# Both attention sections put in the order of the program text on all five engines of an encoder kernel

## The chip, the core and the metric

The kernel runs on one core of one Trainium2 chip. The core has five engines with an instruction queue each: TensorE (PE, matmuls and transposes), VectorE (DVE), ScalarE (ACT), GpSimd (POOL) and SyncE (SP, which here does nothing but issue DMAs). Each engine has one queue, and in the trace its instructions start in the order in which the built program has them, so that one that waits for another engine or for a DMA holds up all that stand behind it. The metric is the time of one execution on the device in microseconds (us); lower is better.

## What is computed

Two encoder layers over 1024 tokens of width 1024, and a last RMSNorm. Cut to what matters here:

```python
h = rmsnorm(x, g)
q, k, v, ..., gate = split(h @ w_in)                 # one input projection for all head groups
# layer 0: 6 windowed heads (A), 6 dense heads with rotary positions (B), 4 heads into 256 memory tokens (X)
# layer 1: 6 differential heads (C), 4 memory heads (X)
p  = softmax(q @ k.T / 8 + bias);  y = p @ v         # A (with a sink logit), B, X
p1, p2 = softmax(q1 @ k1.T / 8 + bias), softmax(q2 @ k2.T / 8 + bias)
y  = rmsnorm((p1 - lam * p2) @ v) * c                # C
out = x + (concat(y) * silu(gate)) @ w_out
```

All of it is float32; the kernel splits operands into a high and a low part and sums matmuls of the parts, three for a projection.

## The kernel before

The kernel is written with a recording layer that builds a program, knows which instruction reads and writes which buffer, puts the instructions of each engine in an order by its own estimate of when each is ready, and adds the waits. The order of the program text binds it only where two instructions share data. A buffer tag has a fixed number of slots; a new buffer waits until the slot's last readers are done.

The attention of each layer is a list of steps, one for 128 query rows of a head (256 rows for A): in layer 0 8 X steps, 8 B steps of the first head, then 64 steps of B and A in a pattern that is mostly B, B, A; in layer 1 8 X steps and 6 times 8 C steps. `run_steps` writes them as a software pipeline:

```python
for i in range(n + LAG + 1):
    hooks(i)                          # layer 1, C steps: Early.step(), one piece of w_out
    steps[i - 1].hop()                # DMA er<-e: step i-1's softmax copied to a buffer of rounded words
    finish = steps[i].s1()            # PE scores (sb, sa, sc); DVE minimum (mn, or e and mn); ACT exp
    jobs.pull(...)                    # 8 matmuls of a projection (acc, or pre) for each pull; weights of the next job loaded
    ...                               # posts of a C pair: ssqc, then rbcc
    steps[p3].s3()                    # on every second step: PE probabilities by values (ob, oa, oc)
    steps[p2].s2()                    # two or three steps behind: PE transposes (te, ta), ACT high part, DVE low part
    finish()                          # DVE rz; POOL (B, A) or DVE (C) scales e
    jobs.pull(f // 2)
```

The projections are the filler: a job is six pulls, three for each half of the tokens. At the end of a half its result acc is taken out of PSUM by ACT, mostly with DVE behind it, and for q and k by four or eight DMAs ("rows": cq, ck, bq_d, aq_d, bk). At a job's start `load_w` loads the next job's weights in two pieces: DMA wr, DVE wh (the cast at L241), POOL wl (L243). `Early.step` in layer 1 stores the last piece's two parts (DMAs wo..h and wo..l), loads the next (DMA wor) and splits it (ACT wos, POOL wos); it runs in 32 steps. In layer 0 `load_wout` does likewise for 16 pieces (DMA wor, ACT woh, DVE wol), two a step. wr, wor and yr, a token block of the gated heads for the output projection, share two slots. Late in each layer the filler is `pre_run`, which works ahead on that projection; it loads yr, and ACT and DVE split it.

PSUM tags: S has two slots of 1024 columns (scores), T two of 512 (transposes, ssqc, rbcc), A two of 512 (acc, oc, ob, oa, pre). Most DMAs are issued by SP, so SP's order is the order of their issue.

Of the kernel before, what the change touches and what calls it, by code (L numbers as in the profile page):

```python
# [3 lines left out]

# [1 line left out]

# [82 lines left out]
class Jobs:  # L89
# [59 lines left out]
    def drain(self):  # L149
        self.step = 10 ** 9  # L150
        while self._advance():
            pass


@with_exitstack
def encoder_kernel(ctx, tc, A):
# [76 lines left out]
    def load_w(src, after=None, fast=False):  # L233
        his, los = [], []
        for kh in range(2):
            raw = wp.tile([P, 4, P], F32, tag="wr", name="wr", bufs=2)
            dma(raw, src[:, 4 * kh:4 * kh + 4, :])
            hi = wp.tile([P, 4, P], F32R, tag="wh", name="wh", bufs=4)
            lo = wp.tile([P, 4, P], F32R, tag="wl", name="wl", bufs=4)
            with (tc.issue_after(after[0]) if after else nullcontext()):  # L240
                nc.vector.tensor_copy(hi, raw)  # L241
            with (tc.issue_after(after[1]) if after else nullcontext()):
                (nc.vector if fast else nc.gpsimd).tensor_tensor(out=lo, in0=raw, in1=hi, op=ALU.subtract)  # L243
            his.append(hi)
            los.append(lo)
        return his, los
# [228 lines left out]
    def run_steps(steps, jobs, hooks=None, pace=None):  # L475
        n = len(steps)
        posts = deque()
        p2 = p3 = 0
        finish = None
        for i in range(n + LAG + 1):  # L480
            behind = None
            if jobs is not None:
                jobs.step = i
            if hooks:
                hooks(i)
            if 0 < i <= n and steps[i - 1].hop:
                steps[i - 1].hop()
            if i < n:
                if steps[i].need:
                    jobs.ensure(*steps[i].need)  # L490
                finish = steps[i].s1()
            f = steps[min(i, n - 1)].fill
            if jobs is not None:
                if half[0] and len(wout) >= 8 and jobs.projected():
                    f = pace(i)
                two = f > 1 and p3 < n and p3 + steps[p3].lag + 1 <= i and steps[p3].s3b is not None
                jobs.pull(f - f // 2 - two)
                if hooks:
                    hooks(-1)
            for q in list(posts):  # L500
                q.pop(0)()
                if not q:
                    posts.remove(q)
            if p3 < n and p3 + steps[p3].lag + 1 <= i:
                st, p3 = steps[p3], p3 + 1
                if st.s3 is not None:
                    if st.need3:
                        jobs.ensure(*st.need3)
                    r = st.s3()
                    if r:  # L510
                        posts.append(r)
                    if st.s3b is not None:
                        jobs.pull(two)
                        st.s3b()
            if p2 < n and p2 + steps[p2].lag <= i:
                behind = steps[p2].s2()
                p2 += 1
            if finish:
                with (tc.issue_after(behind.ins) if behind is not None else nullcontext()):
                    finish()  # L520
                finish = None
            if jobs is not None:
                jobs.pull(f // 2)
                if hooks:
                    hooks(-1)
        while posts:
            for q in list(posts):
                q.pop(0)()
                if not q:
                    posts.remove(q)  # L530
# [276 lines left out]
    last = [None]  # L807
# [185 lines left out]
    jobs = Jobs(jl, ld)  # L993
# [73 lines left out]
    steps = x_steps(M, X, gates, 3, lambda h, qb: (Xq[h], qb * P), 0)  # L1067
# [188 lines left out]
        if i < 0:  # L1256
            wout_hook(0, jobs, "g2", r1)

    run_steps(steps, jobs, hooks0, lambda i: i % 4 != 3)
    jobs.drain()  # L1260
    top_stack.close()
    att.close()
    right.close()
# [197 lines left out]
    jobs = Jobs(jl, lambda j: load_w(j["src"], fast=j["tag"] in FAST or j["tag"] == "g7"))  # L1461
# [16 lines left out]
    steps = x_steps(M, X, gates, 3, lambda h, qb: (Xq1[(h, qb // 4)], (qb % 4) * P), 1)  # L1478
# [115 lines left out]
        if i < 0:  # L1594
            wout_hook(1, jobs, "g5", r2)

    run_steps(steps, jobs, hooks1, lambda i: 2)
    jobs.drain()
    left.close()
    st1 = ExitStack()  # L1600
    out_proj(1, None, st1)
# [72 lines left out]
```

## Time and profile before

| | |
|---|---|
| median of 3 runs | 1228.63 us (1226.69 to 1229.92) |
| span of the profiled execution | 1228.9 us |
| instructions | 19560 |
| busy: PE / DVE / ACT / POOL | 1196.5 / 801.1 / 663.1 / 436.3 us |
| layer 0: X and first B head, then B and A mixed | about 70 to 205 us, 205 to 515 us |
| layer 1: X, then C | about 621 to 677 us, 677 to 1158 us |

The page gives the profiled execution by its span alone; it lies within the runs shown, 0.3 us over their median. Times are from the start of the span. A row of the timeline has the start, the duration, the engine, the source line, the operation, output<-inputs, shapes and a count of equal neighbours; "x2" rows are merged. Matmuls overlap in their pipeline, so a row of 0.40 us for 512 columns stands for about 0.23 us of the engine, which the distance of the starts shows. SPq is SP's queue: issues of DMAs.

### The profile page before, as it was taken

The page shows a single profiled execution, that of the slowest core. Times are in us where ns is not written, and L with a number is a line of the kernel's source. Part 1 is how long each engine was busy: PE and PEld are TensorE (multiplying, and loading weights), DVE is VectorE, ACT ScalarE, POOL GpSimd, SP SyncE. Part 2 cuts the span into 40 slices and gives each one's busy share as a digit, 9 for nine tenths or more (in the row PEclk, how much of TensorE's full clock was granted, in tenths as well). Part 3 has the DMA queues.
Part 4 walks back from the last instruction along what each step waited for, and adds up shares of the span by engine and source line. Part 5 has one row for each costly group of instructions (what it writes and reads, how often), then busy time and mean ns, then how long its engine had stood idle before and what let it go on. Part 6 is the DMA issues. An engine that isn't in the chain of part 4 may idle for free.

```text
span 1228.9 us, 19560 instructions
## 1 busy us (share of the span) xinstructions
PE 1196.5 (97%) x6614; PEld 988.4 (80%) x6614; DVE 801.1 (65%) x1495; ACT 663.1 (54%) x1477; POOL 436.3 (36%) x414
## 2 busy tenths in 40 slices
PE   6999999999999999999999999999999999999997
PEld 5788888888888777888888777777787777777886
DVE  5547665377778878635365866766767767667544
ACT  6248754366667766636157744555545454445332
POOL 5023365366665455437112222333143231301100
PEclk9999999999999999999999999999999999999999
DMA  6664445545465565457645445355363452468354
GB/s 257 200 194 147 163 172 163 166 160 207 163 233 209 208 227 191 151 196 237 186 158 156 153 146 164 121 183 163 124 187 125 153 171 105 149 212 285 121 192 155
DMA packets 114304, 216.70 MB, mean 176 GB/s; under 512 B 13302, under 2 KB 47478, under 8 KB 114204
## 3 DMA queue, kind: packets, MB, share of 16 engines
q1 hardware_dynamic: 114060, 215.25, 52.5%
q8 instruction: 53, 0.87, 0.3%
q14 instruction: 47, 0.39, 0.1%
q10 hardware_dynamic: 144, 0.20, 0.0%
HBM read 87.71 MB, written 39.86 MB: 104 GB/s over the span
## 4 chain that ended last, share of the span: by engine, by line
PE 47%; DVE 2%; DMA 1%; issue 1%; ACT 1%; POOL 0%; POOLq 0%; SPq 0%; DVEq 0%; ACTq 0%
PE acc L329 24%; PE po L702 5%; PE oc L1545 3%; PE sc L1505 3%; PE te L580 3%; PE sc L1514 2%; PE pre L702 2%; PE oc L1547 2%; DMA wr<-in_w_in 1%; PE ssqc L1563 1%; PE ox L656 0%; PE rbcc L1576 0%; PE tv L439 0%; PE sx L543 0%; DVE e L1520 0%
## 5 line engine op out<-in xcount | busy, mean ns | idle before, releaser
L329 PE MATMUL acc<-h,wh 128*128 128x512 f32 x1536 | 499.5, 398 | 1.6 <-DVE h L351 0.8
L329 PEld LDWEIGHTS acc<-h,wh 128*128 128x128 f32 x1536 | 282.4, 188 | 65.7 <-issue 7.9
L329 PE MATMUL acc<-h,wl 128*128 128x512 f32 x768 | 303.8, 396 | 1.5 <-POOL wl L243 1.2
L243 POOL TENSOR_TENSOR wl<-wr,wh 128x512 fp32r<-128x512 f32 x94 | 124.8, 1329 | 286.3 <-DVE wh L241 155.0
L1523 ACT ACTIVATE e<-e,mn 128x1024 f32<-128x1024 f32 x96 | 110.0, 1148 | 117.0 <-DVE mn L1520 116.9
L329 PEld LDWEIGHTS acc<-h,wl 128*128 128x128 f32 x768 | 144.3, 188 | 34.9 <-issue 4.4
L1114 POOL TENSOR_TENSOR e<-e,rz 128x1024 f32<-128x1024 f32 x48 | 91.6, 1910 | 84.2 <-DVE rz L1113 57.8
L1520 DVE CUSTOM_DVE_ANT_0 e<-sc,toep 128x1024 f32<-128x1024 f32 x96 | 113.5, 1218 | 8.0 <-PE sc L1514 7.3
L580 PEld LDWEIGHTS te<-identr,er 128*128 128x128 f32 x896 | 92.2, 143 | 18.8 <-PE sa L543 2.2
L580 PE MATMUL te<-identr,er 128*128 128x128 f32 x896 | 99.9, 246 | 4.3 <-DVE O L1578 1.4
L348 DVE TENSOR_TENSOR PT<-te,PT 128x512 fp32r<-128x512 f32 x112 | 74.3, 687 | 42.8 <-ACT PT L347 39.2
L241 DVE CAST wh<-wr 128x512 fp32r<-128x512 f32 x112 | 58.2, 522 | 42.9 <-PE acc L329 17.3
L348 DVE TENSOR_TENSOR PTl<-te,PTh 128x512 fp32r<-128x512 f32 x112 | 74.0, 684 | 9.4 <-ACT PTh L347 8.9
L1545 PE MATMUL oc<-PT,v 128*128 128x512 f32 x192 | 69.8, 403 | 0.7 <-DVE ckl L1420 0.7
L1532 DVE SCALAR_TENSOR_TENSOR e<-e,mr 128x1024 f32<-128x1024 f32 x48 | 66.3, 1381 | 1.5
L347 ACT CAST PT<-te 128x512 fp32r<-128x512 f32 x112 | 62.7, 589 | 7.2 <-PE te L580 6.7
L347 ACT CAST PTh<-te 128x512 fp32r<-128x512 f32 x112 | 62.2, 586 | 7.9 <-PE te L580 7.1
L702 PE MATMUL po<-woh,yh 128*128 128x512 f32 (+1 forms) x172 | 65.7, 382 | 0.0
L702 PE MATMUL po<-woh,yl 128*128 128x512 f32 (+1 forms) x172 | 65.5, 381 | 0.0
L702 PE MATMUL po<-wol,yh 128*128 128x512 f32 (+1 forms) x172 | 65.3, 380 | 0.0
L1105 DVE TENSOR_REDUCE mn<-sb 128x1 f32<-128x1024 f32 x48 | 58.3, 1216 | 7.0 <-PE sb L543 6.6
L350 ACT ACTIVATE yh<-yr 128x256 fp32r<-128x256 f32 (+2 forms) x56 | 24.0, 447 | 66.2 <-DMA yr<-ysc 37.5
(211 smaller groups left out, 2358.7 us busy)
## 6 DMA issues: line engine op xcount, KB each, us to landing
er<-e SPq DMA_DIRECT2D x112, 512.0 KB, 3.0
wr<-in_w_in SPq DMA_DIRECT2D x96, 256.0 KB, 3.0
ysc<-gy SPq DMA_DIRECT2D x16, 512.0 KB, 2.7
cq<-sg SPq DMA_DIRECT2D x64, 128.0 KB, 2.5
ck<-sg SPq DMA_DIRECT2D x48, 128.0 KB, 2.3
er<-e SPq DMA_DIRECT2D x12, 384.5 KB, 2.6
xpsc<-xh SPq DMA_DIRECT2D x18, 256.0 KB, 2.6
xr<-xpsc SPq DMA_DIRECT2D x9, 512.0 KB, 3.6
```

The source lines that it names most:

```text
L243: (nc.vector if fast else nc.gpsimd).tensor_tensor(out=lo, in0=raw, in1=hi, op=ALU.subtract)
L329: lastmm[0] = nc.tensor.matmul(acc, a, b[:, k, c0:c0 + n], start=(i == 0), stop=(i == 23))
L347: nc.scalar.copy(hi, src)
L348: return nc.vector.tensor_tensor(out=lo, in0=src, in1=hi, op=ALU.subtract)
L580: nc.tensor.transpose(to[:, i * P:(i + 1) * P], e[0][:, k * P:(k + 1) * P], idt)
L702: lastmm[0] = nc.tensor.matmul(acc, a, b, start=(start and n == 0), stop=(stop and n == 2))
L1105: nc.vector.tensor_reduce(out=mn, in_=Sp, op=ALU.min, axis=AX.X)
L1114: nc.gpsimd.tensor_tensor(out=et, in0=et, in1=rz.to_broadcast([P, 1024]), op=ALU.mult)
L1520: nc.vector.tensor_tensor_reduce(out=et, in0=Sp, in1=toeps[h][:, w0:w0 + 1024], scale=1.0, scalar=BIG, op0=ALU.add, op1=ALU.min, accum_out ...
L1523: nc.scalar.activation(et, et, AF.Exp, bias=mn[:, m:m + 1], scale=-1.0, accum_out=z[:, m:m + 1])
L1532: nc.vector.scalar_tensor_tensor(out=es[0], in0=es[1], scalar=c, in1=es[0], op0=ALU.mult, op1=ALU.add)
L1545: nc.tensor.matmul(acc, V[:, kt, 0, :], ph.both[:, kt, :], start=(kt == 0), stop=(kt == 7), skip_group_check=True)
```

## The change

A new context manager goes around the steps and the drain of the jobs in both layers. It takes all instructions recorded inside it and, for each of the five engines, ties every one to the preceding one of the same engine. The tie is an order alone, with no semaphore. Nothing is added to the computation or taken from it, and instructions outside the two sections stay free, among themselves and to move into a section.

```diff
+@contextmanager
+def in_order(tc, engines):
+    bb = tc.nc.cur_bb.bb
+    seen = bb.instructions[-1]
+    yield
+    traced = bb.instructions
+    start = next(k for k in reversed(range(len(traced))) if traced[k] is seen) + 1
+    last = {}
+    for i in traced[start:]:
+        if i.engine not in engines:
+            continue
+        if i.engine in last:
+            tc.add_manual_dep(i, last[i.engine].name,
+                              mybir.DependencyInfo(mybir.DependencyClass.NoSync, mybir.DependencyReason.DATA),
+                              reason="in_order")
+        last[i.engine] = i
...
-    run_steps(steps, jobs, hooks0, lambda i: i % 4 != 3)
-    jobs.drain()
+    with in_order(tc, (mybir.EngineType.PE, mybir.EngineType.Activation, mybir.EngineType.Pool, mybir.EngineType.DVE, mybir.EngineType.SP,)):
+        run_steps(steps, jobs, hooks0, lambda i: i % 4 != 3)
+        jobs.drain()
...
-    run_steps(steps, jobs, hooks1, lambda i: 2)
-    jobs.drain()
+    with in_order(tc, (mybir.EngineType.PE, mybir.EngineType.Activation, mybir.EngineType.Pool, mybir.EngineType.DVE, mybir.EngineType.SP,)):
+        run_steps(steps, jobs, hooks1, lambda i: 2)
+        jobs.drain()
```

Lines of the changed kernel lie 18 to 22 further down than those of before (L348 is L366, L1105 is L1123). Buffer numbers are those of the program text, so a larger number was written later.

First place: VectorE in two B steps of layer 0. mn_3485 is the row minimum of the next step's scores sb_3480; PTl_3415 and PTl_3416 are the low parts of this step's transposes; rz_3475 belongs to the softmax of mn_3444; gy is a gate. Before:

```order
L1105 TENSOR_REDUCE mn_3444<-sb_3439 128x1
L241 CAST wh_3500<-wr_3498 128x512
L460 SCALAR_TENSOR_TENSOR gy_3167<-gy_3167,acc_3328 128x512
L348 TENSOR_TENSOR PTl_3415<-te_3461,PTh_3413 128x4x128
L1105 TENSOR_REDUCE mn_3485<-sb_3480 128x1
L348 TENSOR_TENSOR PTl_3416<-te_3468,PTh_3414 128x4x128
L1113 RECIPROCAL rz_3475<-z_3447 128x1
```

The same place now:

```order
L1123 TENSOR_REDUCE mn_3444<-sb_3439 128x1
L478 SCALAR_TENSOR_TENSOR gy_3167<-gy_3167,acc_3328 128x512
L366 TENSOR_TENSOR PTl_3415<-te_3461,PTh_3413 128x4x128
L366 TENSOR_TENSOR PTl_3416<-te_3468,PTh_3414 128x4x128
L1131 RECIPROCAL rz_3475<-z_3447 128x1
L1123 TENSOR_REDUCE mn_3485<-sb_3480 128x1
L259 CAST wh_3494<-wr_3492 128x512
L259 CAST wh_3500<-wr_3498 128x512
```

The next step's minimum moved behind both low parts and the reciprocal of the step before, and both casts, which wait for DMAs, to the place in the text where the job begins.

Second place: SyncE in layer 1, between two C steps. wor_9399 and wor_9487 are the w_out pieces of two following steps, er_9404 the softmax copy of a step, the cq rows are a finished half of a q projection. Before:

```order
L175 DMA wo10h_117<-wos_9277 128x256
L175 DMA wo10l_118<-wos_9277 128x256
L175 DMA wor_9399<-in_w_out1 128x256
L175 DMA wor_9487<-in_w_out1 128x256
L175 DMA cq_9391<-sg_9387 64x512
L175 DMA cq_9394<-sg_9387 64x512
L175 DMA cq_9391<-sg_9388 64x512
L175 DMA cq_9394<-sg_9388 64x512
L175 DMA er_9404<-e_9294 128x1024
```

The same place now:

```order
L193 DMA cq_9391<-sg_9387 64x512
L193 DMA cq_9391<-sg_9388 64x512
L193 DMA cq_9394<-sg_9387 64x512
L193 DMA cq_9394<-sg_9388 64x512
L193 DMA wo10h_117<-wos_9277 128x256
L193 DMA wo10l_118<-wos_9277 128x256
L193 DMA wor_9399<-in_w_out1 128x256
L193 DMA er_9404<-e_9294 128x1024
```

The loads wor moved from ahead of the rows, one and two steps early, to behind the rows, where the step that uses them begins.

Third place: ScalarE in the same two C steps; O and sqc are the output of the head pair and its square, PT the high parts of the transposes, e the two exponentials of a step, z2 the reader of ssqc. Before:

```order
L1550 COPY O_9351<-oc_9334 128x256
L347 CAST PT_9358<-te_9360 128x4x128
L347 CAST PT_9359<-te_9367 128x4x128
L1553 ACTIVATE sqc_9354<-O_9351 128x256
L350 ACTIVATE sg_9387<-acc_9312 128x512
L270 CAST wos_9401<-wor_9399 128x256
L1523 ACTIVATE e_9417,mn_9282<-e_9417,mn2_9406 128x1024
L1523 ACTIVATE e_9420,mn_9282<-e_9420,mn2_9406 128x1024
L1567 ACTIVATE z2_9443<-ssqc_9440,es_9356 128x1 x2
```

The same place now:

```order
L1572 ACTIVATE sqc_9354<-O_9351 128x256
L365 CAST PT_9358<-te_9360 128x4x128
L365 CAST PT_9359<-te_9367 128x4x128
L368 ACTIVATE sg_9387<-acc_9312 128x512
L288 CAST wos_9401<-wor_9399 128x256
L1542 ACTIVATE e_9417,mn_9282<-e_9417,mn2_9406 128x1024
L1542 ACTIVATE e_9420,mn_9282<-e_9420,mn2_9406 128x1024
L1586 ACTIVATE z2_9443<-ssqc_9440,es_9356 128x1 x2
```

The square moved ahead of the two high parts; wos stood ahead of the exponentials before as well, and still does.

More of the change, by code (lines that the diff above doesn't have):

```diff
@@ L2 @@
 from collections import deque
-from contextlib import ExitStack, nullcontext
+from contextlib import ExitStack, contextmanager, nullcontext
 import numpy as np
```

## The prediction

> **What bounds the kernel now.** I read the page's busy shares first, then who waited for whom on PE and on SP, then the stage of each loop in the timeline.
>
> ```profile
> PE 1196.5 (97%) x6614; PEld 988.4 (80%) x6614; DVE 801.1 (65%) x1495; ACT 663.1 (54%) x1477; POOL 436.3 (36%) x414
> PE sa L543 <- DVE mn L1184: 3.7, 3, 2.2
> PE ob L1127 <- ACT PTh L347: 1.4, 1, 1.4
> SPq L175 <- POOL e L1114: 102.1, 42, 7.9
> SPq L175 <- DVE e L1532: 78.6, 32, 9.8
> ```
>
> PE is the bound: 32 us of 1228.9 idle, over the whole program, so a new order can gain hardly more than 1 to 2%. Its longest waits inside attention are 2.2 and 1.4 us. SP, in contrast, waits often and long (42 times for POOL, 32 for DVE), and what stands behind such a wait is late. Before, loads were put ahead of these waits.
>
> Small waits of PE are not the whole price. The granted clock in two neighbouring stretches of the windows view (PE busy, PEclk, DMA share, GB/s):
>
> ```profile
> 415.00:420.00 5.00, 3.51 (x19) 0.99 0.92 313
> 420.00:425.00 5.00, 5.00 (x25) 0.67 0.35 104
> ```
>
> After the 1.4 us wait of ob the next stretch runs at 0.67, that is some 3 us at half speed, which loses about 1.4 us more.
>
> [...]
>
> **The change, part by part.** It adds no instruction and no DMA. On PE nearly every row stands as before, a few filler matmuls apart. What moves is DVE, ACT, POOL and SP. POOL's wl goes behind the scaling of e; its weights are first read six pulls later, so I cost it at nothing (6 times 1.3 us if that cover were gone). Stores and loads with readers whole steps away (ysc, xpsc, xh, toep, ab) cost nothing for the same reason. The rest I price by loops: in each I follow the durations until the first instruction of the next step can start.
>
> *1. B and A steps of layer 0.* Now mn of the next step stands behind both PTl and rz of this one.
>
> ```profile
> 259.24 1.21 DVE L1105 TENSOR_REDUCE mn<-sb 128x1 f32<-128x1024 f32 x1
> 284.89 1.21 DVE L1105 TENSOR_REDUCE mn<-sb 128x1 f32<-128x1024 f32 x1
> ...
> 300.22 0.37 ACT L471 COPY yt<-oa 64x256 f32<-64x256 f32 x1
> 300.62 1.07 ACT L347 CAST PTh<-te 128x512 fp32r<-128x512 f32 x2
> 301.23 1.29 DVE L348 TENSOR_TENSOR PTl<-te,PTh 128x512 fp32r<-128x512 f32 x2 [0.19 <-ACT PTh L347]
> 303.00 0.60 ACT L459 ACTIVATE gy<-acc 128x512 f32<-128x512 f32 x1 [1.31 <-PE acc L329]
> 305.10 1.21 DVE L1105 TENSOR_REDUCE mn<-sb 128x1 f32<-128x1024 f32 x1
> 306.73 1.21 ACT L1110 ACTIVATE e<-sb,mr,nrq 128x1024 f32<-128x1024 f32 x1
> 307.83 0.19 ACT L1110 ACTIVATION_READ_ACCUMULATOR e<-sb,mr,nrq 128x1 f32 x1
> 308.05 0.17 DVE L1113 RECIPROCAL rz<-z 128x1 f32<-128x1 f32 x1 [1.07 <-ACT e L1110]
> 310.04 0.61 DVE L1184 CUSTOM_DVE_ANT_0 e<-sa,ab,nsink 128x384 f32<-128x384 f32 x1
> 310.75 0.62 ACT L1188 ACTIVATE e<-e,mn 128x385 f32<-128x385 f32 x1 [1.22 <-DVE mn L1184]
> 313.16 0.86 ACT L347 CAST PTa<-ta 128x384 fp32r<-128x384 f32 x2
> 313.67 1.02 DVE L348 TENSOR_TENSOR PTa<-ta,PTa 128x384 fp32r<-128x384 f32 x2
> ```
>
> From the first to the second row lie two triples B, B, A: 25.65 us, 12.8 for one, paced by PE. In text order, for B: from mn (305.10) to the end of exp (308.02) 2.9; high and low parts of te, from 300.62 to 302.52, 1.9; rz 0.17: 5.0, with a yt copy in every second 5.4. A: minimum 0.7, two exponentials of 0.8 each, yt 0.4, PTa from 313.16 to 314.69 1.5, rz 0.17: 4.3. One eviction of acc in three steps, 0.6. Sum 15.3 for a triple, 2.5 more, 0.83 a step. PE no longer paces it; the DVE and ACT round does. About 35 such steps pass before the w_out loads begin: +29. It would be zero if PE's own slot waits already made this round, and it does not, since the triple takes 12.8.
>
> *2. Loads inside these steps.* The casts stand right where the job starts, behind mn and ahead of yt and PTl, and their DMAs behind er, which waits for POOL.
>
> ```profile
> 317.86 1.89 POOL L1114 TENSOR_TENSOR e<-e,rz 128x1024 f32<-128x1024 f32 x1 [2.35 <-issue]
> ...
> er<-e SPq DMA_DIRECT2D x112, 512.0 KB, 3.0
> wr<-in_w_in SPq DMA_DIRECT2D x96, 256.0 KB, 3.0
> wor<-in_w_out SPq DMA_DIRECT2D x16, 256.0 KB, 3.4
> wor<-in_w_out SPq DMA_DIRECT2D x32, 128.0 KB, 2.3
> ```
>
> From rz on: POOL ends at 2.05 (a start 0.15 after rz), er issued by 2.6, wr 1 and 2 at 2.6 and 2.9, landed at 5.9; second cast over at 6.5; yt and PTl to 8.0 instead of 5.2. Five such job starts at 2.8: +14. Before, DMA and cast were early and hidden.
>
> *3. w_out pieces and token blocks in layer 0.* ACT's woh stands ahead of yt and PTh and waits for wor: issued 2.6, landed 6.0, woh 0.63 to 6.7, then PTh and PTl to 9.0, and the second piece's DVE part behind rz: 9.7 instead of 5.2, +4.5 in 8 steps: 36. Five steps with yr, priced like wor: +3.3 each, 16. This stretch already ran slower than the round of part 1,
>
> ```profile
> L175 SPq DMA_DIRECT2D wor<-in_w_out x48: 327/333/719, 352.5 to 994.9; - x48
> L543 PE MATMUL sa<-ak,q x48: 274/404/689, 240.9 to 507.7; 128*128 128x384 f32 x36, 128*128 128x256 f32 x12
> ```
>
> (29 steps from 352.5 to 507.7, 5.35 each), so 8 of the 52 are paid already: +44.
>
> *4. X steps and the first B head.* Three pulls a step (24 matmuls, 5.5 us) cover most; rope rows ahead of wr hold DVE for up to 8 us. I take +15 over 24 steps, between 0 and 50, nearest to zero since PE has a whole step of filler there.
>
> *5. Layer 1: rows ahead of wor.* The rows of a q half and the next w_out piece, the two pieces' ACT and POOL times, and a step with ssqc:
>
> ```profile
> L270 ACT CAST wos<-wor x32: 395/406/437, 685.7 to 998.0; 128x256 fp32r<-128x256 f32 x32
> L271 POOL TENSOR_TENSOR wos<-wor,wos x32: 729/746/1080, 686.2 to 999.4; 128x256 fp32r<-128x256 f32 x32
> ...
> 741.16 1.07 PE L1505 MATMUL sc<-ck,cq 128*128 128x512 f32 x4
> 744.19 1.16 ACT L1523 ACTIVATE e<-e,mn 128x1024 f32<-128x1024 f32 x1 [3.64 <-DVE mn L1520]
> 745.34 0.58 ACT L350 ACTIVATE sg<-acc 128x512 fp32r<-128x512 f32 x1
> 745.95 2.63 SPq L175 DMA_DIRECT2D cq<-sg  x4
> 746.95 0.51 PE L580 MATMUL te<-identr,er 128*128 128x128 f32 x4
> 747.13 0.41 ACT L1567 ACTIVATE z<-ssqc,es 128x1 f32<-128x1 f32 x2
> 749.61 0.43 SPq L175 DMA_DIRECT2D wo10h<-wos  x1
> 750.09 0.43 SPq L175 DMA_DIRECT2D wo10l<-wos  x1
> ```
>
> From the step's sc: acc evicted by 0.9, rows to 3.5, wo h and l to 4.4, wor landed 6.8, wos to 7.2; behind it on ACT both exponentials (1.35 each with their read) to 9.9 and z to 10.4. The second te needs the T slot of ssqc, which z frees; PE is there at 6.2 (747.4). Wait 4.2. In the next step, with oc, the second wr needs the slot that POOL's wos frees at 8.0: landed 11.1, cast 11.5, O scaled 12.0, T slot late by 2.2. The following ssqc step starts 0.8 later on DVE: 5. Then the casts stand ahead of the next head's minimum: exponentials and eviction end some 5 us after PE needs its A slot. 16.4 for a head, three heads, and 7 in the first: +56. Covers lost: a wor one step ahead.
>
> *6. Other pairs of layer 1.* In the row above te came 0.2 ahead of z: no slack. sqc ahead of PT costs 0.43 plus the wait for DVE, and two acc matmuls between the te groups now come later: 1 us in each of some 16 pairs, and 4 at yr: +20.
>
> *7. Half clock after long waits.* 14 waits of part 5 at 1.4, 20; layer 0, where the round hides part, 8 (0 to 25): +28.
>
> Sum 29+14+44+15+56+20+28 = 206; 1228.9+206 = 1435. The span equals the median within 0.3, so no correction.
>
> **Rivals.**
> *Queues run ahead.* If SP and ACT mostly run ahead of PE by a step, DMAs land in time, and parts 2, 3, 5 and 7 shrink to a fifth (28), part 4 to zero; 1 and 6 stay: 1229+29+28+20, 1306. For it: fill is deep, three pulls a step in layer 1. Against: er's waits of up to 9.8 us ahead of the loads.
> *Waits multiply.* A late step makes the next eviction, its rows and the next load late too, so that parts 2, 3, 5 and 7 (142) cost twice: 1577. Against it: a round with no load or rows gives the time back to SP, and half of the steps are such.
> *Not slower.* The text order keeps PE's groups whole. Were half of PE's 32 idle us to go with the scheduler's order and nothing to come instead: 1213. It decides if every wor and wr lands before its reader's turn, that is if SP is less than one step late everywhere; the 4.2 us of part 5 and the 12.8 against 15.3 of part 1 speak against it, PE's 97% for its being small.
>
> **How the numbers follow.** My forecast has 0.75, queues that run ahead 0.13, waits that multiply 0.06, not slower 0.06, split evenly between a gain and no change; a difference of 0.3% (4 us) can hardly be told from none. So faster 0.03, same 0.03, slower 0.94. The bounds: parts 1, 4 and 7 at zero give 1363; part 4 at 50, part 7 at 45 and parts 3 and 5 half larger give 1537. Below, the range takes in the first rival (1306), above it ends a little over the bound: 1295 to 1550. Left out are the second and third rival and a little of the forecast's own spread.
>
> **What would show it.** Right: PE falls from 97% to about 83%; mn rows of layer 0 about 15 us for a triple; ACT waits for DMA wor in layer 1 and te waits there for z; half clock stretches after them; busy times of DVE, ACT and POOL unchanged. Part 2: DVE idle before the cast until DMA wr. Part 3: ACT idle before woh until DMA wor. Wrong: if ssqc steps keep about 9 us, SP was not late; if PE's idle time in layer 0 is spread in short waits without wor, part 3 was too large.

## The result, and the profile after

The changed kernel takes 1633.59 us in the median of 4 runs (1630.21 to 1638.91), against 1227.95 us before: a ratio of 1.331 (95% interval 1.328 to 1.334), 406 us more. The forecast was 1435 us in a range up to 1550: the direction was right, the size was not, and the time lies 84 us beyond the range. The profiled execution has a span of 1637.1 us, 408 more than before.

The busy shares and the clock row of the changed kernel's page (40 equal slices, tenths of full speed, 9 is 90% or more):

```profile
PE 1317.7 (80%) x6614; PEld 1073.7 (66%) x6614; DVE 811.0 (50%) x1495; ACT 665.0 (41%) x1477; POOL 435.7 (27%) x414
PEclk9978989789878767878999989898898988999899
```

PE runs the same 6614 matmuls but is busy 121 us longer (1317.7 against 1196.5), at a mean granted clock of 0.888 instead of 0.996: of the 121, the half clock accounts for 115 or all, by the two estimates in the last section. Its idle time grew from 32 to 319 us, 287 more. Together these are the 408. DVE, ACT and POOL are as busy as before, within 10 us.

Next the windows view by stage (length; busy time of PE, PEld, DVE, ACT, POOL; mean PEclk, DMA share, GB/s): X steps of layer 0, first B head (with the first two B steps of the mix), B and A mixed from the first A step on, C steps of layer 1. Before:

```profile
70.20:139.80 69.60, 68.96 (x411) 58.81 (x410) 43.45 (x76) 54.28 (x145) 22.80 (x20) 1.00 0.54 178
139.80:240.90 101.10, 101.10 (x546) 85.58 (x544) 55.94 (x91) 46.78 (x88) 50.42 (x39) 1.00 0.47 157
240.90:508.00 267.10, 258.59 (x1605) 223.60 (x1605) 205.97 (x417) 186.40 (x444) 156.17 (x140) 0.99 0.56 200
673.30:1137.10 463.80, 461.02 (x2437) 363.08 (x2435) 328.26 (x596) 237.56 (x484) 123.84 (x128) 1.00 0.50 163
```

The changed kernel:

```profile
70.40:167.10 96.70, 74.31 (x383) 63.84 (x382) 43.50 (x72) 52.12 (x139) 21.99 (x18) 0.84 0.39 120
167.10:299.90 132.80, 112.79 (x576) 94.36 (x574) 61.53 (x96) 48.63 (x93) 50.03 (x39) 0.93 0.36 118
299.90:758.90 459.00, 308.16 (x1600) 257.99 (x1599) 200.89 (x418) 190.24 (x443) 158.76 (x141) 0.80 0.33 118
939.40:1535.10 595.70, 510.27 (x2437) 397.06 (x2435) 333.77 (x593) 236.31 (x487) 122.91 (x130) 0.90 0.39 127
```

By stage: +27, +32, +192 and +132; layer 1's X steps and the tail make up the other 25. The mixed stage lost most, at a mean clock of 0.80, and there the forecast had about 95 (parts 1 to 3 and its 8 of part 7).

Who waited for whom in the changed kernel (us in all, times, longest; its lines are some 18 higher than before):

```profile
PE sa L561 <- DVE mn L1202: 117.9, 23, 11.6
PE te L598 <- DVE O L1597: 30.8, 12, 4.5
PE te L598 <- ACT z L1586: 29.4, 17, 4.6
DVE wh L259 <- DMA wr<-in_w_in: 172.4, 79, 8.3
ACT wos L288 <- DMA wor<-in_w_out: 93.6, 17, 7.2
SPq L193 <- POOL e L1132: 246.9, 48, 11.3
SPq L193 <- DVE e L1551: 162.3, 24, 13.3
```

The last six are of the kind that was forecast: SP waits ahead of `er`, casts wait for `wr`, ScalarE for `wor`, `te` for `z`. The first is not: before it was 3.7 us, and PE's row had been costed at nothing. One place shows both (rows of the timeline, then two rows of the windows view):

```profile
405.02 0.15 DVE L1131 RECIPROCAL rz<-z 128x1 f32<-128x1 f32 x1
405.09 1.20 DVE L1123 TENSOR_REDUCE mn<-sb 128x1 f32<-128x1024 f32 x1
405.31 1.89 POOL L1132 TENSOR_TENSOR e<-e,rz 128x1024 f32<-128x1024 f32 x1 [2.98 <-issue]
407.08 0.34 PE L561 MATMUL sa<-akl,q 128*128 128x384 f32 x1
407.23 0.47 SPq L193 DMA_DIRECT2D er<-e  x1
407.75 1.35 SPq L193 DMA_DIRECT2D wr<-in_w_in  x2
411.43 0.43 DVE L259 CAST wh<-wr 128x512 fp32r<-128x512 f32 x1 [5.13 <-DMA wr<-in_w_in]
412.17 1.36 DVE L259 CAST wh<-wr 128x512 fp32r<-128x512 f32 x1 [0.31 <-DMA wr<-in_w_in]
414.65 0.59 DVE L1202 CUSTOM_DVE_ANT_0 e<-sa,ab,nsink 128x384 f32<-128x384 f32 x1
415.31 0.69 PE L561 MATMUL sa<-ak,q 128*128 128x384 f32 x1 [7.89 <-DVE mn L1202]
...
407.20:415.30 8.10, 0.22 (x2) 0.00 (x0) 3.51 (x8) 2.02 (x6) 2.90 (x4) 0.76 0.38 130
415.30:418.40 3.10, 3.10 (x8) 2.63 (x9) 0.62 (x2) 1.42 (x4) 2.16 (x2) 0.53 0.00 0
```

`er` waits for POOL, `wr` stands behind `er`, the two casts wait for `wr`, and the A step's first minimum (414.65) stands behind them. This is part 2 of the prediction, row by row (rz to end of second cast 8.5 us, forecast 6.5). But PE stands too. An A step has two halves (j = 0, 1) that share one score tile, and the second half's scores wait for the first half's minimum. In the text each half is written whole:

```python
for j in range(2):
    qk(Sp[:, j, c:c + n], ...)                                   # sa
    nc.vector.tensor_tensor_reduce(..., accum_out=mn[:, j:j+1])  # e, mn
    nc.scalar.activation(...)                                    # exp
```

PE's row at such a step, before and now (from the programs' order):

```
L580 MATMUL te<-identr,er 128x128 x8          L598 MATMUL te<-identr,er 128x128 x8
L543 MATMUL sa<-ak_2295,q 128x384             L561 MATMUL sa<-ak_2295,q 128x384
L543 MATMUL sa<-akl_2297,q 128x384            L561 MATMUL sa<-akl_2297,q 128x384
L329 MATMUL acc<-h,wh 128x512 x2              L561 MATMUL sa<-ak_2295,q 128x256
L329 MATMUL acc<-h,wl 128x512                 L561 MATMUL sa<-akl_2297,q 128x256
L329 MATMUL acc<-h,wh 128x512 x2              L347 MATMUL acc<-h,wh 128x512 x2
L543 MATMUL sa<-ak_2295,q 128x256             L347 MATMUL acc<-h,wl 128x512
L543 MATMUL sa<-akl_2297,q 128x256            L347 MATMUL acc<-h,wh 128x512 x2
```

Here five filler matmuls lay between the halves before, and now none does. In the trace of before 4 to 27 matmuls lie between the halves of each of the 24 A steps; in that of the changed kernel there is none in 23 of them. These are the "few filler matmuls" that the prediction waved through.

### The profile page after: what moved, and what is told of

Its sections match the earlier page's. It is cut to its first block, busy times and chain, and to the rows that moved or that the text cites. A ratio compares the mean times of both kernels' runs of the same rounds, so it can differ in the third digit from the quotient of the medians.

```text
span 1637.1 us, 19519 instructions
## 1 busy us (share of the span) xinstructions
PE 1317.7 (80%) x6614; PEld 1073.7 (66%) x6614; DVE 811.0 (50%) x1495; ACT 665.0 (41%) x1477; POOL 435.7 (27%) x414
## 5 line engine op out<-in xcount | busy, mean ns | idle before, releaser
L347 PE MATMUL acc<-h,wh 128*128 128x512 f32 x1536 | 534.8, 425 | 12.7 <-DVE gy L478 5.8
L347 PEld LDWEIGHTS acc<-h,wh 128*128 128x128 f32 x1536 | 309.2, 205 | 90.1 <-issue 12.1
L347 PE MATMUL acc<-h,wl 128*128 128x512 f32 x768 | 323.8, 422 | 0.9 <-POOL wl L261 0.9
L598 PE MATMUL te<-identr,er 128*128 128x128 f32 x896 | 108.7, 260 | 91.9 <-DVE O L1597 30.8
L347 PEld LDWEIGHTS acc<-h,wl 128*128 128x128 f32 x768 | 156.8, 204 | 38.6 <-issue 4.4
L259 DVE CAST wh<-wr 128x512 fp32r<-128x512 f32 x112 | 76.5, 684 | 181.0 <-DMA wr<-in_w_in 172.4
L561 PE MATMUL sa<-ak,q 128*128 128x384 f32 (+1 forms) x48 | 25.5, 531 | 117.9 <-DVE mn L1202 117.9
L366 DVE TENSOR_TENSOR PT<-te,PT 128x512 fp32r<-128x512 f32 x112 | 74.1, 687 | 86.6 <-ACT PT L365 85.6
L561 PEld LDWEIGHTS sa<-ak,q 128*128 128x128 f32 x48 | 11.4, 238 | 125.8 <-DVE mn L1202 125.8
L366 DVE TENSOR_TENSOR PTl<-te,PTh 128x512 fp32r<-128x512 f32 x112 | 72.0, 684 | 22.5 <-ACT PTh L365 21.8
L491 POOL TENSOR_TENSOR gy<-yt,gy 64x256 f32<-64x256 f32 x48 | 35.2, 733 | 173.3 <-DVE yt L490 173.0
L289 POOL TENSOR_TENSOR wos<-wor,wos 128x256 fp32r<-128x256 f32 x32 | 27.7, 865 | 185.7 <-ACT wos L288 185.7
L1524 PE MATMUL sc<-ck,cq 128*128 128x512 f32 x192 | 60.2, 437 | 7.3 <-ACT e L650 5.1
```

The source lines that it names most:

```text
L347: lastmm[0] = nc.tensor.matmul(acc, a, b[:, k, c0:c0 + n], start=(i == 0), stop=(i == 23))
L366: return nc.vector.tensor_tensor(out=lo, in0=src, in1=hi, op=ALU.subtract)
L598: nc.tensor.transpose(to[:, i * P:(i + 1) * P], e[0][:, k * P:(k + 1) * P], idt)
L1524: full = nc.tensor.matmul(Sps[m][:, c], C[h][(m, qb // 4)][:, qc], C[h]["k"][m][:, c], start=True, stop=False)
```

## The experiments

Theory A: PE's own row carries a large part (the second half's scores behind the first half's minimum). Theory B: late DMA issue on SP carries it. A third, R, is for what was left: a round of DVE and ACT, each behind the other. Each kernel was compared with the kernel before on the same chip.

| kernel | tied engines | edit | us | ratio to before (95%) |
|---|---|---|---|---|
| changed | all five | | 1633.6 | 1.331 (1.328 to 1.334) |
| e1_no_pe | ACT, POOL, DVE, SP | | 1567.6 | 1.280 (1.275 to 1.285) |
| e2_no_sp | PE, ACT, POOL, DVE | | 1461.5 | 1.192 (1.189 to 1.195) |
| e3_sa_pair | all | both scores first | 1569.2 | 1.280 (1.276 to 1.284) |
| e4_pe_only | PE | | 1308.6 | 1.066 (1.061 to 1.071) |
| e5_late_casts | all | casts at step's end | 1630.0 | 1.329 (1.326 to 1.332) |
| e6_wor_ahead | all | `wor` one step ahead | 1605.3 | 1.310 (1.307 to 1.313) |
| e7_three | all | e3, e5 and e6 | 1505.7 | 1.227 (1.225 to 1.230) |
| e8_before_sa | none | both scores first | 1221.7 | 0.997 (0.995 to 0.998) |
| e9_no_sp_sa_pair | PE, ACT, POOL, DVE | both scores first | 1381.1 | 1.126 (1.124 to 1.128) |
| e10_loads_loose | all, but loads of weights | | 1490.7 | 1.215 (1.213 to 1.217) |
| e11_sp_only | SP | | 1271.0 | 1.037 (1.035 to 1.040) |
| e12_no_pe_sp | ACT, POOL, DVE | | 1364.5 | 1.111 (1.109 to 1.114) |
| e13_dve_only | DVE | | 1265.1 | 1.031 (1.029 to 1.032) |
| e14_act_only | ACT | | 1253.1 | 1.022 (1.020 to 1.023) |
| e15_pool_only | POOL | | 1231.9 | 1.004 (1.003 to 1.005) |
| e16_dve_act | DVE, ACT | | 1370.8 | 1.116 (1.114 to 1.119) |
| e17_loads_sa | all, but loads of weights | both scores first | 1411.1 | 1.151 (1.147 to 1.154) |

### PE's row: e1, e3, e4, e8

e1 and e4 edit only the tuple of engines given to `in_order`, as all runs of "tied engines" do:

```diff
-    with in_order(tc, (PE, Activation, Pool, DVE, SP)):
+    with in_order(tc, (Activation, Pool, DVE, SP)):       # e1; e4 has (PE,)
```

e3 (and, on the kernel before, e8) splits the loop of the A step:

```diff
 for j in range(2):
     qk(Sp[:, j, c:c + n], ...)
+for j in range(2):
     nc.vector.tensor_tensor_reduce(...)
     nc.scalar.activation(...)
```

e1:

> The changed kernel with the instructions of TensorE alone left to the scheduler again; ScalarE, GpSimd, VectorE and SyncE stay in the order of the text. Theory A (TensorE's own order was the cost that the prediction put at nothing: the second half's score matmuls wait on the first half's minimum, 117.9 us in 23 waits of the chain of waits after, 3.7 us before): a large part of the 405 us comes back, 120 to 180 us, so 1455 to 1515 us, and the waits of `sa` on `mn` are under 15 us. Theory B (late DMAs and the order on SP carry it: `cast wh` waits 172.4 us for `wr`, `wos` 93.6 us for `wor`): little comes back, under 40 us, so over 1590 us, since the casts and pieces still wait as they did.

e3:

> The changed kernel with one edit of the text: in an A step the score matmuls of both halves are written ahead of both minima, so that no score matmul stands behind a minimum of its own step; all five engines stay in the order of the text. Theory A: the 117.9 us of waits of `sa` on `mn` go, and with them some of the half clock behind each (median `sa` matmul 542 ns after, 404 ns before); PE then stops later, at the next step's `PTl` or `mn`, so that 80 to 150 us come back: 1485 to 1555 us. Theory B (late loads and DVE's row set the pace, TensorE only shows it): PE stops as long at another matmul of the step, under 30 us come back, over 1600 us.

e4:

> The kernel before with the instructions of TensorE alone tied to the order of the text; the other four engines are left to the scheduler. Theory A in its strong form (the order of TensorE's row alone costs the steps of the text): 1330 to 1420 us, with waits of `sa` on `mn` over 60 us. In its weak form (the row costs only where VectorE comes late to the first half's minimum, which it does behind casts that wait for a DMA): 1235 to 1290 us, with `sa` waits of 10 to 40 us. Theory B: no change within 1 per cent, 1220 to 1240 us.

e8:

> The kernel before, all engines left to the scheduler, with the one edit that writes both halves' scores ahead of both minima. Theory A: before waited 3.7 us in `sa` on `mn` since the scheduler put matmuls between the halves, so the edit is worth 0 to 5 us: 1222 to 1231 us. The rival: the text's order sets the scheduler's priorities, and the edit brings scores earlier and holds back others, 10 to 25 us slower.

e1 gave back 66 us and e3 64 us, both less than theory A had asked for and more than theory B. In e3 the wait of `sa` on `mn` is gone from the list, and the whole gain lies in the mixed stage (459.0 to 393.7 us). In time that one text edit is worth as much as all of PE's freedom while the other rows stay fixed, but not in the same places: of e1's gain 34 us lie in the mixed stage, 19 in the C steps. e4, with PE alone tied, fell between its two forms: 82 us, with 30.8 us of `sa` waits:

```profile
PE sa L561 <- DVE mn L1202: 30.8, 23, 2.3
```

The same 23 waits, at most 2.3 us long instead of 11.6: how long PE stands there is set by how late DVE is. But only some 30 of e4's 82 us lie in the mixed stage; 27 lie in the C steps and 20 in the X steps and the first B head, so PE's row costs outside the A steps too. No run takes that part further apart. e8 gave 4.5 us to the kernel before, where the scheduler had not hidden the wait wholly: a small gain, at the upper end of what was expected, and the one version faster than both kernels.

### SP's row: e2, e5, e6, e10, e11

e10 leaves the loads `wr` and `wor` out of the tie, and nothing else:

```diff
-        if i.engine not in engines:
+        if i.engine not in engines or i.name in LOOSE:   # LOOSE: names of the wr and wor DMAs
             continue
```

e5 and e6 edit the text. In e5 `load_w` issues its DMAs as before and puts the casts (`wh`, `wl`) in a list that is emptied behind `finish()`. In e6 `Early.step` fetches the next piece:

```diff
 def step(self):
     self.store()
-    raw = wp.tile([P, 512], F32, tag="wr", name="wor", bufs=2)[:, 0:256]
-    dma(raw, w_out...)                        # this step's piece
+    raw, ... = self.raw                       # loaded in the last step
+    self.fetch()                              # the next one, into a slot of its own class
     nc.scalar.copy(hi, raw)
```

e2:

> The changed kernel with the DMA issues on SyncE left to the scheduler; the four compute engines stay in the order of the text. Theory A (TensorE's order): the waits of `sa` on `mn` stay near 118 us and the time stays above 1580 us. Theory B (the row of issues on SP, in which a load of weights stands behind stores that wait, 246.9 us for POOL and 162.3 us for DVE in SP's own waits): loads are issued earlier, the 172.4 us of casts that wait for `wr` and the 93.6 us of pieces that wait for `wor` shrink to under a third, and the time falls by 150 us or more, under 1480 us.

e10:

> The changed kernel in which SyncE's row is tied as well, but for the loads of weights (`wr` of a job, `wor` of the output weights), which the scheduler may issue as soon as their slot is free; the other four engines have the very rows of the changed kernel. Theory B1 (what SyncE's order costs is that a load of weights is issued behind the `er` copies of the step, each of which waits for its exponentials): nearly all of the 172 us that came back with SyncE's order left free come back here too: 1460 to 1490 us, `cast wh` waits for `wr` under 45 us, `wos` for `wor` under 10 us. Rival B2 (the late `er`, `q` and `yr` transfers carry it, the weights' loads are only where it is seen): under 60 us come back, over 1575 us.

e5:

> The changed kernel with one edit: a job's load of weights issues its two DMAs at the start of the step as before, but the casts and remainders of the loaded tiles (VectorE's `wh`, GpSimd's `wl`) are written at the end of that step, behind the step's own minimum, exponentials and transposes. All engines stay in the order of the text. Theory A (TensorE's row waits on minima that stand behind casts): the 172.4 us in which casts wait for `wr` fall under 40 us, and 60 to 120 us of the time come back: 1515 to 1575 us. Theory B (loads that come late whatever the place of the cast): the waits for `wr` fall as well, but the consumers of `wh` wait in their place, under 30 us come back, over 1600 us.

e6:

> The changed kernel with one edit: each `wor` piece of the output weights of layer 1 is loaded one step ahead of the multiply that uses it, into a slot of its own class rather than the two slots that the `wr` loads share. All engines stay in the order of the text. The prediction's part 5 (layer 1 rows wait at the head of a step for `wor`): ScalarE's waits of `wos` on `wor`, 93.6 us in 17, fall under 20 us and 40 to 80 us come back: 1555 to 1595 us. The rival (ScalarE's wait covers work that stands still for TensorE anyway): the waits go but under 20 us come back, over 1610 us.

e11:

> The kernel before with SyncE's DMA issues alone tied to the order of the text; the four compute engines are left to the scheduler. If a late load costs only where the rows of the compute engines are fixed too, so that work queues behind the cast that waits: 1228 to 1270 us. If the late issue costs by itself: 1300 to 1400 us, with `cast wh` waiting over 100 us for `wr`.

e2 gave back 172 us, so theory B holds for the larger share, beside A: the `sa` waits stayed, at 88.5 us. e10 is the clean form, since the four compute engines have the very rows of the changed kernel: 143 us come from nothing but where SP issues loads of weights. B1 was right, 1 us above its range. Its waits:

```profile
DVE wh L262 <- DMA wr<-in_w_in: 31.3, 20, 4.9
PE sa L564 <- DVE mn L1205: 101.9, 23, 13.4
```

The casts' wait fell from 172.4 to 31.3 us, and that of `wos` from 93.6 to 2.6 us. The 29 us between e10 and e2 come with SP's other DMAs (`er`, `q`, `yr`, rows).

e5 brought 4 us, which is within the spread of the runs, as its rival had it. The casts' wait for `wr` did fall, from 172.4 to 22.9 us, but other waits took its place:

```profile
409.62 1.15 DVE L265 CAST wh<-wr 128x512 fp32r<-128x512 f32 x2 [1.49 <-DMA wr<-in_w_in]
410.69 0.61 DVE L1220 CUSTOM_DVE_ANT_0 e<-sa,ab,nsink 128x384 f32<-128x384 f32 x1
411.36 0.69 PE L579 MATMUL sa<-ak,q 128*128 128x384 f32 x1 [5.66 <-DVE mn L1220]
...
PE sa L579 <- DVE mn L1220: 114.7, 23, 10.9
ACT wos L302 <- DMA wor<-in_w_out: 141.6, 24, 9.0
```

The end of a step is where the next one begins: the casts again stand right ahead of a minimum, `sa` waits nearly as long as in the changed kernel (114.7 against 117.9 us), `wos` waits longer for `wor` (141.6 against 93.6) and `te` longer for `z` (66.3 against 29.4). Moving the reader of a late load did not help here; issuing the load earlier did. e6 took the waits of `wos` on `wor` (93.6 us) away and got 28 us for them, between its two expectations: most of that wait cost nothing by itself. e11, SP alone tied, costs 45 us, 1 us over its first case:

```profile
DVE wh L259 <- DMA wr<-in_w_in: 48.2, 51, 3.4
```

With the compute engines' rows free the casts still wait, but 48 us in all instead of 172: late issue costs more where the rows behind the cast are fixed too.

### Both together: e7, e9, e17

e7:

> The changed kernel with three edits together: both halves' scores ahead of both minima, the casts of a job at the end of its step, `wor` one step ahead. All engines stay in the order of the text. If the three costs lie one behind another on the path: 180 to 260 us come back, 1375 to 1455 us. If they lie beside one another (one engine's lateness seen at three places): no more than the largest of the three alone and 30 us.

e9:

> The changed kernel with SyncE left to the scheduler and both halves' scores ahead of both minima; the other four engines in the order of the text. The two alone gave 172 and 64 us. If the late loads and TensorE's wait on the first half's minimum lie one behind the other on the path (the minimum stands behind casts that wait for loads), the second is worth less once the first is gone, 88.5 us of waits of `sa` being left: 1385 to 1420 us. If each uncovers the other, as the three edits together gave 128 us for 64, 28 and 4 alone: 1340 to 1380 us.

e17:

> The changed kernel with the weights' loads free on SyncE and the scores of both halves ahead of both minima; all else in the order of the text. The two alone gave 143 and 64 us. If they add: 1420 to 1435 us. If the late casts hid part of TensorE's wait (an A step that starts late for its cast waits either way), the pair gives more than the sum, as with SyncE wholly free (172 and 64 alone, 253 together): 1395 to 1415 us. A steps without loads should then fall from 8.4 us to about 4.2.

The causes uncover each other. e3's edit is worth 64 us in the changed kernel, but 80 once the loads are early (1490.7 to 1411.1 in e17, its second case; 1461.5 to 1381.1 in e9). e9 so ended between its two cases, 1 us above the second. e7 has 128 us for parts that gave 64, 4 and 28, between its cases too: more than beside one another, less than the 180 of the first. In e7 the issue of `wr` is as late as in the changed kernel; that this makes the difference is likely, not shown. An A step in e10, and then one in e17, whose scores of both halves stand together:

```profile
337.43 0.34 PE L564 MATMUL sa<-akl,q 128*128 128x384 f32 x1
341.45 0.15 DVE L1134 RECIPROCAL rz<-z 128x1 f32<-128x1 f32 x1
341.52 0.60 DVE L1205 CUSTOM_DVE_ANT_0 e<-sa,ab,nsink 128x384 f32<-128x384 f32 x1
342.18 0.58 PE L564 MATMUL sa<-ak,q 128*128 128x256 f32 x1 [4.42 <-DVE mn L1205]
...
342.18:348.10 5.92, 5.92 (x19) 5.14 (x20) 1.23 (x4) 1.31 (x4) 4.01 (x3) 0.50 0.74 250
```

```profile
338.07 0.34 PE L564 MATMUL sa<-ak,q 128*128 128x384 f32 x1
338.25 0.33 PE L564 MATMUL sa<-akl,q 128*128 128x384 f32 x1
338.42 0.63 PE L350 MATMUL acc<-h,wh 128*128 128x512 f32 x2
342.63 0.47 DVE L1210 CUSTOM_DVE_ANT_0 e<-sa,ab,nsink 128x256 f32<-128x256 f32 x1
```

In e10 no load is late here, yet PE stands 4.4 us behind DVE's ordinary row (evictions, two low parts, rz), and then runs 5.9 us at half clock. In e17 its filler follows the scores at once. From an A step's first minimum to the next step's (median of 23): 5.6 us before, 8.9 in the changed kernel, 8.4 in e10, 4.3 in e17. The prediction's 4.3 for an A step was the round of DVE and ACT, and holds only where PE is not held.

### What was left, the round of DVE and ACT: e12 to e16

e12:

> The kernel before with ScalarE, GpSimd and VectorE tied to the order of the text, TensorE and SyncE left to the scheduler. This is the prediction's part 1 and 6 (the round of VectorE and ScalarE, the order of the rest) without the late loads and without TensorE's row. If these two were all that the prediction missed, its own terms for parts 1, 4 and 6 (29, 15 and 20 us) stand: 1270 to 1310 us. If the round of VectorE and ScalarE was itself mis-sized: 1340 to 1400 us.

e13:

> The kernel before with VectorE alone tied to the order of the text. Theory R (a round: each of VectorE and ScalarE stands behind the other, so that fixing one lets the other's free row fill in): 1235 to 1265 us. Rival D (VectorE's row by itself: the minimum of the next step behind the remainders and reciprocals of this one): 1310 to 1365 us, nearly all of the 138 of the run with three engines tied.

e14:

> The kernel before with ScalarE alone tied to the order of the text. Theory R (a round of two engines): 1235 to 1265 us. Rival S (ScalarE's row by itself: casts and evictions behind exponentials that wait for a minimum): 1310 to 1365 us.

e15:

> The kernel before with GpSimd alone tied to the order of the text. The prediction priced GpSimd's row at nothing: 1220 to 1235 us. The rival (remainders `wl` and scalings of `e` late on GpSimd hold `er` and the weights): over 1250 us.

e16:

> The kernel before with VectorE and ScalarE tied to the order of the text, GpSimd, TensorE and SyncE free. Theory R: most of the 138 us that three tied engines cost, 1320 to 1360 us, and at least 40 us more than the two single runs add up to. If one row carries it (rivals D or S): within 20 us of the dearer single run. If GpSimd's row is the missing part: under 1300 us.

With PE and SP free, 138 us of the loss are there already (e12), where parts 1, 4 and 6 said 64. DVE alone costs 38, ACT alone 26, POOL 4.5; DVE and ACT together cost 143, which is 80 more than their sum and all that e12 has. e13, e14 and e15 ended in the ranges of theory R and of the prediction, e16 11 us above R's. Waits of ACT on the minimum of B before, in e13, e14 and e16, and of DVE on ACT's high part in e16:

```profile
ACT mr L1109 <- DVE mn L1105: 41.5, 31, 3.3
...
ACT mr L1127 <- DVE mn L1123: 27.8, 21, 3.3
...
ACT mr L1127 <- DVE mn L1123: 61.7, 30, 3.7
...
ACT mr L1127 <- DVE mn L1123: 102.9, 47, 4.4
DVE PTl L366 <- ACT PTh L365: 24.1, 21, 3.0
```

With one row fixed ACT's waits are within some 20 us of those of before; with both fixed, ACT waits for DVE's minimum in nearly every one of the 48 B steps, and DVE's waits for ACT's `PTh` have grown too, from 8.9 us before to 24.1. That is the round, but it is not shown to be all of the 143 us. In the mixed stage e16 loses 85 us where e9, with the same two rows and those of PE and POOL tied and both halves' scores first, loses 48: a B step takes 5.3 us in both (median), an A step 6.3 in e16 and 4.2 in e9. So a part of e16's loss probably lies in where a free PE row puts the scores of the A steps; this was not tested apart.

## Why the prediction was wrong, point by point

**The step that failed** is "On PE nearly every row stands as before, a few filler matmuls apart". Those fillers were the cover of a wait: 64 to 80 us (e3; e17 against e10; e9 against e2), forecast nothing. Outside the A steps that row costs as well, some 47 us when it is tied alone (e4). The chain of part 1 followed DVE and ACT from step to step and never asked what PE waits for inside an A step, though the row that names it, `sa` on `mn`, was the longest of the two PE waits quoted. Beside it, the half clock of layer 0 (part 7) and the price of part 4 were far too small, and part 3 took as paid what was not:

*Part 1* (+29). In e9 PE's wait and the late loads are gone, and what is left is this round with the rest of the fixed rows; its mixed stage is 48 us longer than before (315.0 against 267.1). The first 35 steps from the first A step on, as many as the prediction counted, take 4.78 us each there and 4.22 before: 20 us where it had 29, since a triple takes 14.4 (median of the first twelve in e9, and in e17) and not 15.3. The 26 steps behind them take 5.59 against 4.53: 28 us more that the prediction had not counted, as it took the round for paid there. Its "29 steps from 352.5 to 507.7, 5.35 each" are 35 steps of 4.4 us in the trace of before, where the first `wor` was issued some seven steps ahead of its reader. So "8 of the 52 are paid already" was not so.

*Parts 2 and 3* (+58) were near in sum: with PE's wait out of the way, freeing the loads of weights shortens the mixed stage by 56 us (e3 to e17, 393.7 to 337.3), and freeing SP's other DMAs, `yr` among them, by 22 more (e9, 315.0).

*Part 4* (+15, 0 to 50) was too small: the X steps and the first B head took 74 us more (27, 32 and 15). Late loads have 27 of it, what e10 gives back there; 46 remain. "A whole step of filler" did not cover the rows: in these stages PE's row alone costs 20 us (e4), DVE and ACT together 22 (e16).

*Part 5* (+56) was right in kind and nearly so in size. A step of the changed kernel of the kind that it followed (rows of a q half, a piece of w_out, ssqc), whose `sc` starts at 1135.33:

```profile
1136.16 2.48 SPq L193 DMA_DIRECT2D cq<-sg  x4
1138.68 0.59 SPq L193 DMA_DIRECT2D wo10h<-wos  x1
1139.31 0.44 SPq L193 DMA_DIRECT2D wo10l<-wos  x1
1139.85 0.40 SPq L193 DMA_DIRECT2D wor<-in_w_out  x1
1142.60 0.40 ACT L288 CAST wos<-wor 128x256 fp32r<-128x256 f32 x1 [6.47 <-DMA wor<-in_w_out]
1142.91 1.14 ACT L1542 ACTIVATE e<-e,mn 128x1024 f32<-128x1024 f32 x1
1145.18 0.39 ACT L1586 ACTIVATE z<-ssqc,es 128x1 f32<-128x1 f32 x2
1145.63 0.75 PE L598 MATMUL te<-identr,er 128*128 128x128 f32 x4 [3.97 <-ACT z L1586]
```

`wor` is issued behind the rows and the stores, `wos` waits for it, the exponentials and `z` stand behind `wos`, and `te` waits 4.0 us for `z`; the forecast wait was 4.2. With the loads free the C stage falls by 82 us (595.7 to 513.7 in e10). Of these 50 are PE's idle time (85.4 to 35.4 us, length less busy time), to be set beside the 56, and 32 its busy time (510.3 to 478.3), beside the 20 that part 7 had for these waits.

*Part 6* (+20): with loads early the C stage is still 48 us longer than before (512.1 in e17 against 463.8), with whatever half clock is left in it. PE's row alone costs 27 us there (e4), DVE and ACT together 26 (e16).

*Part 7* (+28): PE's busy time rose by 121 us, 49 of it in the C stage and 50 in the mixed stage, where the forecast had 8; the X steps and the first B head have 21 more. The price hung on the waits of part 5, but layer 0 had half clock too: 28 stretches at 0.50 begin in it between 70 and 759 us. In 17 of them, or in the 3.4 us ahead, PE's longest wait is one of `sa` on `mn` (2.8 to 11.6 us), in the other 11 another one of 1.7 to 7.8 us. How much of the 121 would have been idle time at full clock was not measured apart.

One chain of runs takes the difference of the two profiled executions, 408 us, apart. In the mixed stage it goes by 459.0 (changed), 393.7 (e3), 337.3 (e17), 315.0 (e9) and 267.1 us (before): 65 for PE's wait at `sa`, 56 for the loads of weights, 22 for SP's other DMAs and 48 for the round and the rest. The C stage has 132 (82 with the loads, 50 behind them), the X steps and the first B head 74, the tail 10. The half clock is inside these terms. The shares depend on the order in which the causes are taken away: e3's edit, worth 65 us there as the first, is worth 83 when the loads are free already (420.5 in e10 to 337.3 in e17).

**The rivals.** *Queues run ahead* failed: loads were late nearly everywhere (79 waits of casts). *Waits multiply* (1577) came nearest in time but not by its mechanism: the loads of weights cost 143 to 158 us (e10; e17 against e3), all of SP's row 172 to 188 (e2; e9 against e3), where the forecast for parts 2, 3, 5 and 7 was 142, not double. What multiplied was tying several engines at once. *Not slower* failed.

**What would show it.** PE's share fell to 80% (forecast 83), and ACT's waits for `wor`, `te`'s for `z`, DVE's for `wr` and the half clock all came. The triple takes 14.4 us in e17, not far from the forecast 15.3, but 20 in the changed kernel (medians of the first twelve). The sign against part 3 came in part: of the 188 us by which the steps from the first A step on grew, 88 lie ahead of the first w_out piece. "PE's row stands" had no test in that list; the waits view of PE would have been one.

## What to carry to other kernels

When an order is fixed, look for every wait inside one step that filler covers now, PE's row included: a few matmuls between two halves of one tile were worth 64 to 80 us, and writing both halves' scores first cures it in the text. A load that waits for nothing should not be issued behind stores that wait: freeing such loads brought 143 us, while moving their reader to the end of the step brought 4 and only moved the wait. Two engines that feed each other cost far more with both rows fixed (143 us) than the sum of each alone (63), though not all of that is shown to be their round; price the round, and count every step that it holds in.

## What the runs showed of the hardware

The half clock came in stretches of one unit. In the windows view of the changed kernel, cut finely around the wait shown above, the granted clock falls to 0.50 at 411.4 us, 4.0 us after PE's last matmul and still inside the wait, and is full again at 418.2: 6.8 us, in which PE stood for 3.9 and worked for 2.9. In e10 it falls at 341.3, 3.5 us after the last matmul, and is full again at 348.1: 6.8 us as well, but PE worked for 5.9 of them. In the kernel before, around the 1.4 us wait of `ob`, it is at 0.50 from 419.9 to 423.3: 3.4 us. The whole trace of the changed kernel has 51 such stretches, 366 us of its span (before: 3, 10 us); each but the last, which the end of the program cuts off, lasts 3.41 us or two to six times that, and all of them start a whole number of 3.41 us after the first.

PE was busy in 245 of the 366 us. Two neighbouring matmuls of `acc` start 0.43 us apart inside these stretches and 0.23 us apart outside them (medians of 234 and 1859 pairs). As an estimate, 115 of the 245 us were lost by that ratio, and 122 by the clock of 0.50, to be set beside the 121 by which PE's busy time grew. A wait therefore had no fixed price: reckoned with the 0.50, the same 6.8 us lost about 1.5 us in the one place and 3 in the other, as the wait itself covered more or less of them. The prediction's 1.4 came from a stretch of 3.4 us, which by this reckoning lost 1.7.

Half clock followed where PE had been less busy. The trace of the changed kernel, cut into pieces of 3.41 us in step with these stretches, has 369 pieces at full clock. Behind all 45 in which PE was busy for at most 43% the clock was 0.50 in the next piece, behind 6 of the 17 from 44 to 63%, and behind none of the 307 with more. Of the 107 pieces at half clock, none of the 56 in which PE was busy for up to 82% was followed by full clock, 2 of the 3 from 83 to 85% were, and all of the 48 with more. In the kernel before, the 1.4 us wait lay in a piece with 59%. These are counts of two traces: no run varied PE's share by itself.

In e10 the work at half clock went on for 5.9 us: it began 0.9 us after the fall, so that PE was busy for 74% of the first 3.41 us, and full clock came only after the second.
